# A two-layer encoder trunk on one core: the MLP's second product by seven block products instead of eight

## The chip, the core and the metric

The kernel runs on one NeuronCore of one Trainium2 chip. The metric is the time of one execution on the device in microseconds (us), the median of several runs. Engine names are those of the profile: PE is the matmul engine, PEld its weight loads, DVE the vector engine, ACT the scalar engine, POOL the general engine, SP the engine whose queue issues most transfers. Matmuls add up in eight banks of 128 x 512 floats, which the program names by the tiles `s` (two tiles of two banks), `pj` and `tp` (two banks each).

## What is computed

Two layers over 1024 tokens of width 1024, in 32-bit floats. Each layer has a mixer (layer 0: pooling and a gated recurrence; layer 1: chunked attention), a cross-attention into 256 memory tokens, and an MLP of width 4096, each between two RMSNorms. The change touches the MLP:

```python
def squared_relu_mlp(h, w1, w2):
    a = jax.nn.relu(h @ w1)
    return (a * a) @ w2
...
h = rmsnorm(x, g[4])
x = x + rmsnorm(squared_relu_mlp(h, w_ff1[l], w_ff2[l]), g[5])
```

Here h is 1024 x 1024, w1 is 1024 x 4096 and w2 is 4096 x 1024.

## The kernel before

**Products.** Operands go to PE in the type fp32r, and every operand is split into a high part (ACT casts it) and a low part (DVE subtracts the high part from the source), and one block product is three matmuls: high by high, high by low, low by high (`mm3`, L157; `split`, L170; `wsplit`, L120). All matmuls stand in the profile under L137. A tile of 128 x 1024 floats costs one cast and one subtraction.

**First product of the MLP** (`sevens`, L651). The 32 column tiles of w1 are taken in pairs n = 0 to 15. With the tokens in two halves and the inner dimension in two halves, a pair is a 2 x 2 by 2 x 2 block product. Pairs 1 to 15 are done by seven block products instead of eight (i = 0 to 6, in the order 0, 1, 3, 2, 5, 4, 6; Strassen's method in Winograd's form), each of 12 matmuls; pair 0 by eight (i = 7 to 14), while the sums of token blocks that the seven need are still being built. Those sums are made by `to_set` (L590) and `end_set` (L620) and lie in tiles `S` and, for one of them, in four tiles of the pool `a`. The list `seq` (L757 to L759) writes out the order by hand. `evac` (L738) is what empties the banks: ACT copies (L747), DVE adds (L754), and then relu and square either on ACT in two instructions (L749, L750) or on DVE in one (L755, for i = 1, 4 and 5). A finished pair is two tiles of 128 x 1024 in the pool `a`; ACT's queue writes them to device memory (`ffa`, L752).

**Second product** (L762 to L820). The 32 tiles f of the squared activation are read back in eleven blocks of 2, 3 (eight times), 2 and 4. For each f, `act` (L767) splits the activation tile into `ff` and `wsplit` splits the 128 rows of w2. For each of the eight row tiles tb, and each half n of the 1024 columns, the block's tiles are multiplied in one go, 3 matmuls per f. The result of a block goes by ACT copy (first block, L809) or DVE add (L811) into `y`, 8 tiles of 128 x 1024. In the last block, of four f, each row tile is finished at once: the sum of squares (L241), the gain (POOL, L242), the scale (POOL, L206 and L207), the residual (L244), the next norm (L213, L215) and, in layer 0, transposes for the next stage (L140). The last row tile of the program goes through `finish` (L249).

**What sets the order.** The kernel is written as a stream; a scheduler then orders each engine's instructions and gives out buffers from pools: `h8` (12 tiles of 8 KB per partition), `a` (15 tiles of 4 KB), `raw` (3), `w` (4) and `x` (5). A load waits in SP's queue until its buffer is free, and everything behind it waits too. `piece` (L143) fixes the order of PE's pieces.

## Time and profile before

| | |
|---|---|
| median of 3 runs | 2872.77 us (2872.22 to 2874.97) |
| the profiled execution | 2876.44 us, of which 2874.6 us are the span from the first to the last instruction |
| granted clock of PE, mean | 0.996 |
| PE busy, share of the span | 99% |
| first product of the MLP, layer 0 | from 688 us to 999.5 us |
| second product of the MLP, layer 0 | from 999.5 us to about 1352 us |
| second product of the MLP, layer 1 | from about 2517 us to 2865.2 us |

A group of instructions in the profile has the line, the engine, the operation, the tile written and the tiles read, the shapes and the count; then its busy time and the mean of one in ns; then the engine's idle time ahead of it and who ended it. A window lists the busy time of each engine in a stretch of the span, in brackets the number of instructions, then PE's granted clock, the share of the transfer engines' time and GB/s. Matmuls overlap, so the time of one is read from the distance between them.

### The profile page before, as it was taken

The numbers are of one execution on the slowest core, as the hardware profiler recorded it, in microseconds if no ns is written. First come the engines' busy times: TensorE is split into PE (matmuls) and PEld (weight loads), VectorE is DVE, ScalarE is ACT, GpSimd is POOL, SyncE is SP. The second block draws the span as 40 slices with busy tenths as digits, with TensorE's granted clock in tenths as the row PEclk, the third lists the DMA queues.
The fourth block names the chain that finished last, engine by engine and source line by source line (L and its number), as shares of the span: only waits on it lengthen the run. The fifth ranks groups of instructions, "written<-read, shape, count | busy, mean of one in ns | idle before, by whom it ended". The sixth has DMA issues, their size and how long they took to land.

```text
span 2874.6 us, 36400 instructions
## 1 busy us (share of the span) xinstructions
PE 2832.7 (99%) x13894; PEld 2375.2 (83%) x13894; DVE 1582.5 (55%) x2550; ACT 1131.8 (39%) x2174; POOL 620.3 (22%) x845
## 2 busy tenths in 40 slices
PE   9999999999999999999999999999999999999998
PEld 7888888888888888888888888878888888888887
DVE  4577733356755644555555556544255755645454
ACT  4344523443433421213555566633344433431111
POOL 2233413211000000005555555723211000000003
PEclk9999999999999999999999999999999999999999
DMA  7211632133333432332111111542033333442222
GB/s 194 60 33 35 190 133 88 44 114 114 121 114 118 164 122 88 101 108 92 54 38 38 39 47 44 155 141 96 30 118 115 127 110 104 151 155 88 88 88 88
DMA packets 173934, 283.68 MB, mean 99 GB/s; under 512 B 10416, under 2 KB 117552, under 8 KB 173760
## 3 DMA queue, kind: packets, MB, share of 16 engines
q1 hardware_dynamic: 162096, 243.35, 26.8%
q10 hardware_dynamic: 11664, 38.02, 3.5%
q8 instruction: 109, 1.79, 0.3%
q14 instruction: 65, 0.53, 0.1%
HBM read 214.74 MB, written 66.58 MB: 98 GB/s over the span
## 4 chain that ended last, share of the span: by engine, by line
PE 91%; DVE 3%; ACT 2%; POOL 2%; DMA 1%; issue 1%; SPq 0%; DVEq 0%; POOLq 0%; ACTq 0%
PE s L137 43%; PE pj L137 33%; PE tp L137 11%; PE tp L140 4%; DVE x L244 0%; POOL w L127 0%; DVE p L1180 0%; ACT a L125 0%; ACT zT L174 0%; DVE a L175 0%; ACT a L174 0%; POOL a L127 0%; POOL st L207 0%; POOL o L999 0%; DMA x<-in_w_o_att_dram 0%
## 5 line engine op out<-in xcount | busy, mean ns | idle before, releaser
L137 PE MATMUL pj<-hT,w 128*128 128x512 f32 x2640 | 656.0, 398 | 0.4 <-DVE hT L175 0.4
L137 PEld LDWEIGHTS pj<-hT,w 128*128 128x128 f32 x2640 | 481.6, 188 | 95.1 <-issue 1.9
L137 PE MATMUL s<-a,ff 128*128 128x512 f32 x2376 | 547.0, 389 | 0.4 <-ACT s L241 0.4
L137 PEld LDWEIGHTS s<-a,ff 128*128 128x128 f32 x2376 | 445.6, 188 | 93.8 <-ACT s L241 0.9
L137 PE MATMUL s<-S,w 128*128 128x512 f32 x1440 | 341.1, 389 | 0.0
L137 PEld LDWEIGHTS s<-S,w 128*128 128x128 f32 x1440 | 270.1, 188 | 56.3 <-ACT a L747 0.3
L137 PE MATMUL s<-a,zT 128*128 128x512 f32 x1280 | 308.9, 393 | 3.9 <-POOL a L127 3.3
L242 POOL TENSOR_TENSOR a<-y,x 128x1024 f32<-128x1024 f32 x15 | 41.8, 2786 | 1249.2 <-DVE y L811 1249.0
L137 PEld LDWEIGHTS s<-a,zT 128*128 128x128 f32 x1280 | 240.5, 189 | 56.3 <-POOL a L127 5.5
L811 DVE TENSOR_TENSOR y<-y,s 128x1024 f32<-128x1024 f32 x123 | 149.8, 1218 | 185.9 <-PE s L137 185.7
L127 POOL TENSOR_TENSOR w<-raw,w 128x1024 fp32r<-128x1024 f32 x75 | 185.7, 2477 | 240.9 <-ACT w L125 226.5
L770 ACT CAST ff<-x 128x1024 fp32r<-128x1024 f32 x52 | 53.0, 1051 | 322.8 <-PE s L137 321.1
L137 PE MATMUL pj<-a,ff 128*128 128x512 f32 x696 | 164.4, 389 | 0.0
L175 DVE TENSOR_TENSOR a<-tp,a 128x256 fp32r<-128x256 f32 (+2 forms) x272 | 113.5, 422 | 81.1 <-ACT a L174 77.0
L137 PEld LDWEIGHTS pj<-a,ff 128*128 128x128 f32 x696 | 130.7, 188 | 27.1
L125 ACT CAST w<-raw 128x1024 fp32r<-128x1024 f32 x92 | 96.6, 1050 | 130.4 <-PE pj L137 74.3
L137 PE MATMUL tp<-a,a 128*128 128x256 f32 (+1 forms) x1016 | 138.9, 279 | 5.9 <-DVE a L175 3.9
L137 PEld LDWEIGHTS tp<-a,a 128*128 128x128 f32 x1016 | 133.6, 191 | 13.0 <-DVE a L175 7.1
L1152 POOL TENSOR_SCALAR qd<-a 64x256 fp32r<-64x256 f32 x256 | 102.6, 401 | 149.3 <-PE s L137 134.7
L174 ACT CAST a<-tp 128x256 fp32r<-128x256 f32 (+2 forms) x272 | 99.5, 371 | 77.3 <-PE tp L140 47.7
L683 DVE TENSOR_TENSOR w<-a,w 128x512 fp32r<-128x512 f32 x124 | 85.6, 691 | 78.4 <-ACT w L682 78.2
L129 DVE TENSOR_TENSOR a<-raw,a 128x1024 fp32r<-128x1024 f32 x75 | 92.0, 1230 | 59.6 <-PE s L137 43.7
(227 smaller groups left out, 4094.7 us busy)
## 6 DMA issues: line engine op xcount, KB each, us to landing
raw<-in_w_ff_dram SPq DMA_DIRECT2D x96, 512.0 KB, 3.9
ffa<-a ACTq DMA_DIRECT2D x64, 512.0 KB, 2.8
x<-ffa SPq DMA_DIRECT2D x52, 512.0 KB, 5.1
xs<-x SPq DMA_DIRECT2D x40, 512.0 KB, 2.6
x<-xs SPq DMA_DIRECT2D x40, 512.0 KB, 3.4
raw<-in_w_mem_kv_dram SPq DMA_DIRECT2D x32, 512.0 KB, 4.1
x<-in_w_ff_dram SPq DMA_DIRECT2D x32, 512.0 KB, 3.8
raw<-in_w_qkv_dram SPq DMA_DIRECT2D x24, 512.0 KB, 4.0
```

Source lines behind the costliest of these rows:

```text
L125: nc.scalar.copy(h, raw)
L127: nc.gpsimd.tensor_tensor(l, raw, h, op=ALU.subtract)
L129: nc.vector.tensor_tensor(l, raw, h, op=ALU.subtract)
L137: self.lastpe = self.nc.tensor.matmul(*a, **k).ins
L140: self.lastpe = self.nc.tensor.transpose(out, in_, self.ident).ins
L174: nc.scalar.copy(hi, src)
L175: nc.vector.tensor_tensor(lo, src, hi, op=ALU.subtract)
L242: eng.tensor_tensor(yg, y, gpost, op=ALU.mult)
L683: nc.vector.tensor_tensor(w[:, 1], src, w[:, 0], op=ALU.subtract)
L770: nc.scalar.copy(t[:, 0], raw)
L811: nc.vector.tensor_tensor(yp, yp, pp, op=ALU.add)
L1152: nc.gpsimd.tensor_scalar(ts[-1][r * 64:r * 64 + 64, :], q[hd * 64:hd * 64 + 64, mp * 256:mp * 256 + 256], 1.0, 1.0, op0=ALU.mult, op1=ALU ...
```

## The change

**The second product** is done by seven block products for 28 of the 32 tiles f (14 pairs), and as before for the last four (`REST`). Tokens are halved (m), the 256 rows of w2 of a pair are halved, and the columns are halved. The new `seconds` runs 28 steps: four blocks of 2, 4, 4 and 4 pairs, and in each the seven products in the order 0, 2, 3, 1, 5, 4, 6. A step multiplies four row tiles j, one bank each, by one half of the columns, over all pairs of its block: 24 matmuls in the first block, 48 in the others. The stationary operand is a sum of activation blocks, the moving one a sum of blocks of w2.

**Sums.** Seven tiles `acc` of the pool `h8` hold the running sums from block to block. In each block products 0, 3 and 5 go on adding up in the same banks, and DVE adds those banks to the sums after each of the three (L809). For products 1, 2, 4 and 6, ACT copies the running sum into the banks before the step (L799) and out again after it (L812). In the first block ACT copies all seven out. In the last block DVE adds the sums up into the four quarters of the result, of which the last piece, with its four tiles f, reads a row tile where it read `y` before (L926).

**The activation sums** are made in the first product: at the end of each of the 14 pairs DVE does four more operations of 128 x 512 (L874), and four transfers instead of two write seven blocks of 128 x 512 instead of four (`ffd`, L871 to L877). Relu and square for i = 1 and 5 go from DVE to ACT (L860, L861). The list `seq` has `end_set` one product earlier, ahead of (0, 14).

**Operands of a step**: `load` (two steps ahead) reads one activation tile and, for four of the seven products, one w2 tile per two pairs; `split` (one step ahead) forms the difference of w2 blocks on DVE where there is one (L778) and splits both operands (L174, L175). The whole diff, less the part that removes the old loop and the argument `c` of `finish`:

```diff
+    BLOCKS = (0, 2), (2, 4), (6, 4), (10, 4)
+    REST = range(28, 32)
+    PLACE = 6, 0, 2, 3, 5, 4, 1
+    def seconds(self, W, ops_d, mid):
+        nc = self.nc
+        Wv = W.rearrange("(n q p) d -> p n q d", q=2, p=P)
+        steps = [(b, i) for b in range(len(self.BLOCKS)) for i in (0, 2, 3, 1, 5, 4, 6)]
+        raws, stage, tmp, ops, acc, banks = {}, {}, {}, {}, {}, {}
+        NEED = {0: (0, 0), 2: (0, 1), 3: (1, 1), 1: (1, 0)}
+        unit = (P, 2, 512)
+        def raw(tag, src):
+            if tag == "w":
+                t = self.wp.tile(list(unit), F32, tag="w", name=self.nm("w"))
+            else:
+                t = self.rawp.tile(list(unit), F32, tag="raw", name=self.nm("raw")) if tag == "raw" else self.act(tag, unit)
+            nc.sync.dma_start(t, src)
+            return t
+        def load(b, i):
+            n0, kb = self.BLOCKS[b]
+            if i in NEED:
+                q, m = NEED[i]
+                raws[b, q, m] = [raw(("x", "x", "w", "a")[2 * q + m], Wv[:, n0 + h:n0 + h + 2, q, m * 512:m * 512 + 512])
+                                 for h in range(0, kb, 2)]
+            stage[b, i] = [raw("raw", ops_d[(n0 + h) // 2][:, :, self.PLACE[i], :]) for h in range(0, kb, 2)]
+        def split(b, i):
+            kb = self.BLOCKS[b][1]
+            sh, sl = [self.h8([P, 4, 512], F32R, "sh") for _ in range(2)]
+            ops[b, i] = sh, sl, [], []
+            B = lambda q, m, h: raws[b, q, m][h]
+            for h in range(kb // 2):
+                if i == 2:
+                    tmp[b, h] = self.act("a", unit)
+                if i in (0, 1, 4):
+                    x = B(*{0: (0, 0), 1: (1, 0), 4: (1, 1)}[i], h)
+                else:
+                    x = self.act("a", unit) if i == 5 else tmp[b, h]
+                    y, z = {2: ((0, 1), (0, 0)), 3: ((1, 1), None), 5: ((1, 1), (0, 1)), 6: ((1, 0), None)}[i]
+                    nc.vector.tensor_tensor(x, B(*y, h), B(*z, h) if z else x, op=ALU.subtract)
+                for hi, lo, src in ((sh[:, 2 * h:2 * h + 2], sl[:, 2 * h:2 * h + 2], stage[b, i][h]),
+                                    (self.act("a", unit, F32R), self.act("a", unit, F32R), x)):
+                    self.split(hi, lo, src)
+                ops[b, i][2].append(hi)
+                ops[b, i][3].append(lo)
+        def run(k, b, i):
+            kb, last = self.BLOCKS[b][1], b == len(self.BLOCKS) - 1
+            chain = i in (0, 3, 5)
+            if i not in (3, 5):
+                two = [self.p2() for _ in range(2)] if k % 2 == 0 else [self.p1(p, t) for p, t in ((self.pj, "pj"), (self.tp, "tp")) * 2]
+                banks[k % 2] = two
+            w = 2 if k % 2 == 0 else 1
+            ps = [banks[k % 2][j // w][:, j % w * 512:j % w * 512 + 512] for j in range(4)]
+            wide = [t.rearrange("p (j d) -> p j d", j=w) for t in banks[k % 2]]
+            sums = lambda i: [acc[i][:, w * j:w * j + w, :] for j in range(4 // w)]
+            if b == 0:
+                acc[i] = self.h8([P, 4, 512], F32, "acc")
+            elif not chain:
+                for x, y in zip(wide, sums(i)):
+                    nc.scalar.copy(x, y)
+            sh, sl, th, tl = ops.pop((b, i))
+            first = i == 0 or (b == 0 and not chain)
+            for j in range(4):
+                sj = slice(j * P, j * P + P)
+                with self.piece():
+                    for n in range(kb):
+                        t = [x[n // 2][:, n % 2, :] for x in (th, tl)]
+                        for g, (v, m) in enumerate(((sh, t[0]), (sh, t[1]), (sl, t[0]))):
+                            self.mm(ps[j], v[:, n, sj], m, start=(first and n + g == 0), stop=(n == kb - 1 and g == 2), skip_group_check=not first)
+            add = lambda o, x, y: nc.vector.tensor_tensor(o, x, y, op=ALU.add)
+            for x, y in zip(wide, sums(i)):
+                if b == 0 or (not chain and not (last and i in (1, 4, 6))):
+                    nc.scalar.copy(y, x)
+                elif chain:
+                    add(y, y, x)
+            if last and i in (1, 4, 6):
+                for x, y, z in zip(wide, sums({1: 0, 4: 3, 6: 5}[i]), sums({1: 0, 4: 3, 6: 6}[i])):
+                    add(z, y, x)
+            if last and i in (3, 5):
+                for x, y, z in zip(sums(i), sums(2), sums({3: 3, 5: 2}[i])):
+                    add(z, x, y)
+        for k in range(2):
+            load(*steps[k])
+        split(*steps[0])
+        for k, (b, i) in enumerate(steps):
+            if k + 2 < len(steps):
+                load(*steps[k + 2])
+            if k + 1 < len(steps):
+                split(*steps[k + 1])
+            mid(len(steps) - k)
+            run(k, b, i)
+        return (acc[0], acc[3]), (acc[6], acc[2])
...
         W1, W2 = self.a["w_ff1"][l], self.a["w_ff2"][l]
-        act_d = [self.dp.tile([P, S], F32, name=f"ffa{l}_{f}") for f in range(32)]
+        act_d = {f: self.dp.tile([P, S], F32, name=f"ffa{l}_{f}") for f in self.REST}
+        ops_d = [self.dp.tile([P, 2, 7, 512], F32, name=f"ffd{l}_{m}") for m in range(self.REST[0] // 4)]
         o = {}
         def evac(n, i, ps):
@@ -748,74 +852,84 @@
             elif i in (6, 7, 9, 12, 14):
                 nc.scalar.activation(t, ps, AF.Relu)
                 nc.scalar.activation(t, t, AF.Square)
-                for c in range(2) if i in (6, 14) else ():
-                    nc.scalar.dma_start(act_d[2 * n + c], o.pop((n, c)).rearrange("p j t -> p (j t)"))
             else:
                 nc.vector.tensor_tensor(t, ps, t if i == 4 else o[n, 0][:, 1, :], op=ALU.add)
-                nc.vector.scalar_tensor_tensor(t, t, 0.0, t, op0=ALU.max, op1=ALU.mult)
+                if i == 4:
+                    nc.vector.scalar_tensor_tensor(t, t, 0.0, t, op0=ALU.max, op1=ALU.mult)
+                else:
+                    nc.scalar.activation(t, t, AF.Relu)
+                    nc.scalar.activation(t, t, AF.Square)
+            if i not in (6, 14):
+                return
+            o0, o1 = o.pop((n, 0)), o.pop((n, 1))
+            if 2 * n in self.REST:
+                for c, x in enumerate((o0, o1)):
+                    nc.scalar.dma_start(act_d[2 * n + c], x.rearrange("p j t -> p (j t)"))
+                return
+            d = ops_d[n // 2][:, n % 2]
+            s0, s1 = [self.act("a", (P, 2, 512)) for _ in range(2)]
+            nc.scalar.dma_start(d[:, 0:2], o1)
+            for x, y, z, op in ((s0[:, 0], o0[:, 1], o1[:, 1], ALU.add), (s1[:, 0], o0[:, 0], o0[:, 1], ALU.subtract),
+                                (s0[:, 1], s0[:, 0], o0[:, 0], ALU.subtract), (s1[:, 1], o1[:, 0], s0[:, 1], ALU.subtract)):
+                nc.vector.tensor_tensor(x, y, z, op=op)
+            nc.scalar.dma_start(d[:, 2:4], s0)
+            nc.scalar.dma_start(d[:, 4:6], s1)
+            nc.scalar.dma_start(d[:, 6], o0[:, 0])
         seq = [(0, 8), (0, 7), lambda: self.flush(len(self.pending) - 1), (0, 10), (0, 9), lambda: self.flush(), (1, 0), (1, 1)]
-        seq += [(2, 0), (2, 1)] + [(0, i) for i in range(11, 15)] + [lambda: self.end_set(A), (1, 2), (2, 2), (1, 3), (2, 3)]
+        seq += [(2, 0), (2, 1)] + [(0, i) for i in range(11, 13+1)] + [lambda: self.end_set(A)] + [(0, i) for i in range(13+1, 15)] + [(1, 2), (2, 2), (1, 3), (2, 3)]
         seq += [(1, 5), (2, 5), (1, 4), (1, 6), (2, 4), (2, 6)] + [(n, i) for n in range(3, 16) for i in (0, 1, 3, 2, 5, 4, 6)]
         self.sevens(W1, A, evac, seq)
...
+        fs = self.REST
+        def rest(f):
+            raw = self.wraw(act_d[f], (P, S), True)
+            if f == fs[-1]:
+                t = self.h8([P, 2, S], F32R, "ff")
+                a[f] = t[:, 0], t[:, 1]
+            else:
+                a[f] = [self.act("a", (P, S), F32R) for _ in range(2)]
+            self.split(*a[f], raw)
+            w2[f] = self.wsplit(W2[f * P:(f + 1) * P, :], (P, D), "w" if f == fs[1] else "a", "dve")
+        def mid(left):
+            for f in fs[:2] if left == 2 else fs[2:] if left == 1 else ():
+                rest(f)
+        C = self.seconds(W2, ops_d, mid)
...
+        for tb in range(NT):
+            if tb % 2 == 0:
+                y = self.h8([P, 2, D], F32, "y")
+            x = self.load_x(xsrc, tb)
+            tsl = slice(tb * P, tb * P + P)
+            fin = gpre is None and tb == NT - 1
+            ps = None if fin else self.p2()
+            ph = [ps[:, n * 512:n * 512 + 512] if ps is not None else self.p1(self.pj, "pj") for n in range(2)]
+            with self.piece():
+                for n in range(2):
+                    sl = slice(n * 512, n * 512 + 512)
+                    self.mm3(ph[n], [((a[f][0][:, tsl], a[f][1][:, tsl]), (w2[f][0][:, sl], w2[f][1][:, sl])) for f in fs])
+            yt = y[:, tb % 2, :]
+            c = [C[tb // 4][n][:, tb % 4, :] for n in range(2)]
+            if fin:
+                self.finish(ph, c, yt, x, tb, xdst, gpost)
+                break
+            for n in range(2):
+                nc.vector.tensor_tensor(yt[:, n * 512:n * 512 + 512], c[n], ph[n], op=ALU.add)
```

`order` of the built programs counts 10,654 matmuls of 512 columns before and 10,318 now; all other counts on PE are the same.

**Two places in the engines' order.** The first is DVE in layer 0, at the end of the operand sums of the first product. `L175` writing 128x2x128 is a split of the sum that product (1, 4) reads, `L634` and `L674` are sums, `L683` a split of w1, `w920` before and `w922` now that of (1, 4). Before:

```order
L634 TENSOR_TENSOR a913_5906<-a913_5906,S801_5156 128x512
L683 TENSOR_TENSOR w920_6009<-x865_5630,w920_6009 128x512
L175 TENSOR_TENSOR a910_5903<-a912_5905,a908_5901 128x2x128
L175 TENSOR_TENSOR a911_5904<-a912_5905,a909_5902 128x2x128
L674 TENSOR_TENSOR a929_6119<-raw880_5714 128x512
L683 TENSOR_TENSOR w922_6027<-a898_5840,w922_6027 128x512
L175 TENSOR_TENSOR a910_5903<-a913_5906,a908_5901 128x2x128
L175 TENSOR_TENSOR a911_5904<-a913_5906,a909_5902 128x2x128
L175 TENSOR_TENSOR a910_5903<-a913_5906,a908_5901 128x2x128
L175 TENSOR_TENSOR a911_5904<-a913_5906,a909_5902 128x2x128
L754 TENSOR_TENSOR a919_6007<-s2888_5758,a889_5771 128x512
```

The same place now, where `L874` are the new sums of pair 0 and `L856` is the add that was `L754`:

```order
L874 TENSOR_TENSOR a915_5935<-a874_5655 128x512
L634 TENSOR_TENSOR a912_5867<-a912_5867,S801_5156 128x512
L683 TENSOR_TENSOR w922_5998<-x865_5609,w922_5998 128x512
L175 TENSOR_TENSOR a909_5864<-a911_5866,a907_5862 128x2x128
L175 TENSOR_TENSOR a910_5865<-a911_5866,a908_5863 128x2x128
L683 TENSOR_TENSOR w924_6016<-a898_5821,w924_6016 128x512
L175 TENSOR_TENSOR a909_5864<-a912_5867,a907_5862 128x2x128
L874 TENSOR_TENSOR a914_5934<-a914_5934,a874_5655 128x512
L175 TENSOR_TENSOR a910_5865<-a912_5867,a908_5863 128x2x128
L856 TENSOR_TENSOR a921_5996<-s2888_5737,a889_5750 128x512
L175 TENSOR_TENSOR a909_5864<-a912_5867,a907_5862 128x2x128
L175 TENSOR_TENSOR a910_5865<-a912_5867,a908_5863 128x2x128
```

Three of the new sums (the first stands just above these rows) and one add now stand ahead of the last splits; two instructions of L755 and one of L674 that stood ahead are gone from there. Counted from the add that reads bank `pj` of product (1, 1) to the last of these splits there are 46 instructions of 128 x 512 and 8 small ones before, 47 and 8 now.

The second place is ACT in the middle of the second product of layer 0. Before, in the last blocks, it holds nothing but casts:

```order
L770 CAST ff1345_9577<-raw1344_9575 128x1024
L125 CAST a1347_9582<-raw1346_9580 128x1024
L770 CAST ff1350_9588<-raw1349_9586 128x1024
L125 CAST a1352_9593<-raw1351_9591 128x1024
L770 CAST ff1355_9599<-raw1354_9597 128x1024
L125 CAST a1357_9604<-raw1356_9602 128x1024
```

Now, in the third block: `sh` is the stationary operand of a step (`sh1323` that of product 1, which reads `w1307` and `w1308` too, `sh1331` that of product 5 after it), `acc1161` the sum of product 2, `acc1178` that of product 1, and the banks `pj1317`, `tp1318`, `pj1319`, `tp1320` of product 2 are the banks `pj1339` to `tp1342` of product 1:

```order
L174 CAST a1325_8974<-w1307_8884 128x1024
L174 CAST sh1323_8972<-raw1309_8888 128x1024
L174 CAST a1327_8980<-w1308_8886 128x1024
L812 COPY acc1161_8021<-pj1317_8908 128x512
L799 COPY pj1339_9058<-acc1178_8103 128x512
L174 CAST sh1323_8972<-raw1310_8890 128x1024
L812 COPY acc1161_8021<-tp1318_8909 128x512
L799 COPY tp1340_9059<-acc1178_8103 128x512
L812 COPY acc1161_8021<-pj1319_8910 128x512
L799 COPY pj1341_9060<-acc1178_8103 128x512
L812 COPY acc1161_8021<-tp1320_8911 128x512
L174 CAST sh1331_9040<-raw1321_8968 128x1024
```

Each bank's copy out and the copy of the next sum into it follow each other, bank by bank, and the casts for product 1 stand ahead of the last copies out of product 2, two steps before they are used.

68 lines of the change are left out of this document (13 added, 55 removed).

## Prediction

> **What bounds the kernel now.** First the page: the span, the busy times, and the shares of the chain that ended last.
>
> ```profile
> span 2874.6 us, 36400 instructions
> PE 2832.7 (99%) x13894; PEld 2375.2 (83%) x13894; DVE 1582.5 (55%) x2550; ACT 1131.8 (39%) x2174; POOL 620.3 (22%) x845
> GB/s 194 60 33 35 190 133 88 44 114 114 121 114 118 164 122 88 101 108 92 54 38 38 39 47 44 155 141 96 30 118 115 127 110 104 151 155 88 88 88 88
> PE 91%; DVE 3%; ACT 2%; POOL 2%; DMA 1%; issue 1%; SPq 0%; DVEq 0%; POOLq 0%; ACTq 0%
> ```
>
> PE is busy for 99% of the span and is 91% of the chain; no other engine is over 55%. But these are averages, so next the windows of the MLP: one pair of the first product, the second product up to its last block (layer 0), and the last block with what follows.
>
> ```profile
> core 0: us, PE busy (x) PEld busy (x) DVE busy (x) ACT busy (x) POOL busy (x), PEclk, DMA share, GB/s
> 768.04:787.08 19.04, 19.04 (x86) 15.77 (x85) 11.28 (x17) 6.82 (x12) 0.00 (x0) 1.00 0.34 111
> 996.79:1298.96 302.17, 302.17 (x1333) 250.00 (x1333) 155.74 (x149) 66.08 (x70) 0.00 (x0) 1.00 0.33 110
> 1298.96:1352.00 53.04, 52.65 (x248) 43.48 (x247) 28.47 (x28) 17.04 (x31) 31.58 (x28) 1.00 0.29 101
> ```
>
> In both products PE does not pause at all (302.17 of 302.17 us), its clock is granted in full (1.00), and DVE has 48% and ACT 78% of the second product free. So there a matmul that goes is worth its whole distance to the next, as long as the others keep up. That distance is read from the chain in order of time, where a stretch holds nothing but matmuls:
>
> ```profile
> 1007.67 5.44 PE s L137 x24
> 2816.20 43.53 PE s L137 x192
> ```
>
> 24 matmuls in 5.44 us and 192 in 43.53 us are 0.2267 us each (the 389 ns of a row is their length, overlap and all).
>
> **What PE saves.** Before: 8 row tiles by 2 halves by 32 f by 3 = 1536 matmuls per layer. Now: 14 pairs by 7 products by 4 row tiles by 3 = 1176, and 8 by 2 by 4 by 3 = 192 for the last four f: 1368. That is 168 less per layer, 336 in all, as in the built programs (10,654 less 10,318). 336 x 0.2267 = **76.2 us**. [...]
>
> **What the other engines get.** Durations, from the groups kept apart by shape:
>
> ```profile
> L811 DVE TENSOR_TENSOR y<-y,s 128x1024 f32<-128x1024 f32 x123 | 149.8, 1218 | 185.9 <-PE s L137 185.7
> L129 DVE TENSOR_TENSOR a<-raw,a 128x1024 fp32r<-128x1024 f32 x75 | 92.0, 1230 | 59.6 <-PE s L137 43.7 <-ACT a L125 15.8
> ...
> L771 DVE TENSOR_TENSOR ff<-x,ff 128x1024 fp32r<-128x1024 f32 x52 | 62.0, 1221 | 2.7 <-ACT ff L770 2.3
> L755 DVE SCALAR_TENSOR_TENSOR a<-a 128x512 f32<-128x512 f32 x90 | 61.6, 685 | 0.1
> ...
> L770 ACT CAST ff<-x 128x1024 fp32r<-128x1024 f32 x52 | 53.0, 1051 | 322.8 <-PE s L137 321.1 <-DMA x<-ffa 1.7
> ...
> L811 DVE TENSOR_TENSOR y<-y,pj 128x512 f32<-128x512 f32 x72 | 49.3, 687 | 64.8 <-PE pj L137 64.4
> ...
> L750 ACT ACTIVATE a<-a 128x512 f32<-128x512 f32 x38 | 24.1, 635 | 0.0
> ...
> L747 ACT COPY a<-tp 128x512 f32<-128x512 f32 x30 | 17.6, 588 | 45.5 <-issue 40.1 <-PE tp L137 5.4
> ...
> L241 ACT ACTIVATE s<-y 128x1024 f32<-128x1024 f32 x15 | 15.4, 1024 | 75.0 <-DVE y L811 75.0
> ```
>
> First product, per pair of 19.04 us: DVE gains four operations of 128 x 512 and gives up two of L755: 4 x 0.687 - 2 x 0.685 = +1.4, so 12.7 of 19.04 (67%). ACT takes over relu and square twice, 4 x 0.635 = +2.5, so 9.4 (49%). Both stay under PE, and what covers them is the slack of an engine that is 33% or more idle: they cost nothing. Two more writes per pair go through ACT's queue, where an issue takes:
>
> ```profile
> 747.00 0.33 ACTq L752 DMA_DIRECT2D ffa<-a  x1
> ```
>
> That is +0.7 us of ACT's time per pair (53% with it); behind them stand its casts of w1, made three products (8.2 us) ahead.
>
> The turn from pair 0 to the seven products is where DVE is tight, since the operand sums of `end_set` lie there. DVE and PE by time:
>
> ```profile
> 738.70 1.42 DVE L175 TENSOR_TENSOR a<-a,a 128x256 fp32r<-128x256 f32 x4
> 740.73 2.88 PE L137 MATMUL tp<-a,w 128*128 128x512 f32 x12
> ```
>
> The last four splits end at 740.12, and PE starts the product that reads them, (1, 4), at 740.73: 0.6 us to spare, and somewhat more, as its early matmuls read the first two. In the new order one more operation of 128 x 512 stands ahead of them (47 for 46, so +0.7 at most). I take 0.2 us per layer, between 0 and 0.7; not below 0, since PE does not wait there now.
>
> Second product, a block of four pairs: 7 x 48 matmuls, 76.2 us of PE. DVE: 28 low parts at 1.221, 8 differences at 1.230 and three adds of four banks at 2.44 (two of 1.218) to 2.75 (four of 0.687): 51.3 to 52.3 us, 67 to 69%. ACT: 28 casts at 1.051, four copies out and four in; a copy into banks has no row of its own, and L241 (`s<-y`, also from `y` into banks) with 1.024 per two banks and L747 with 0.588 per bank bound it: 2.05 to 2.35 per product, so 45.8 to 48.2 us, 60 to 63%. The block of two pairs: 38.1 us of PE; ACT has 14 casts and seven copies out, 29.1 to 31.2 us, **76 to 82%**, the fullest stretch of the change.
>
> Do the copies lie on PE's path? PE fills bank 0 in the first quarter of a step (2.72 of 10.88 us) and comes back to it two steps after the step's start: 19.0 us to carry out 1.2 us of copies; for the last bank it is the same. Where no copy in is made (first block), the four row tiles take 5.44 us a step, and a bank has 9.5 us. The order of ACT in the section on the change fits this: out and in follow bank by bank, the casts run ahead of them. I take 0, with the rivals below for the cover being gone.
>
> Transfers: a block of four pairs reads 14 activation and 8 w2 tiles of 512 KB, 11.5 MB in 76.2 us, 151 GB/s, for 110 in the window above and up to 194 in the page's slices. All are queued on SP in about the order of use, and steps are loaded two ahead (21.8 us); landings:
>
> ```profile
> raw<-in_w_ff_dram SPq DMA_DIRECT2D x96, 512.0 KB, 3.9
> ...
> x<-ffa SPq DMA_DIRECT2D x52, 512.0 KB, 5.1
> ```
>
> The pieces are 2 KB instead of 4, which no row prices; even at twice 5.1 us they land in time. I take 0.
>
> The end of each MLP: the last piece of four f is the same 192 matmuls, but its low half of the last w2 tile now stands on DVE between the last adds of sums, and a row tile takes two adds from `s` where one of 1218 did (2 x 0.687, +0.16 us). In layer 0 PE already waits there:
>
> ```profile
> 1340.00 5.76 PE L137 MATMUL s<-a,ff 128*128 128x512 f32 x24 [0.22 <-ACT s L241]
> 1346.80 5.74 PE L137 MATMUL s<-a,ff 128*128 128x512 f32 x24 [0.18 <-ACT s L241]
> ```
>
> so I add 0.16 for each of five row tiles, 0.8 us, in layer 0, and 0.3 us per layer for the turn into the last piece (0 to 1.2, one L129).
>
> **The sum.** -76.2 + 2 x 0.2 + 0.8 + 2 x 0.3 = -74.4 us. The profiled execution took 2876.44 us (span 2874.6 and 1.8 around it) and would take 2802.0. It is 3.7 us above the median of the runs, so the median goes from 2872.8 to **2798.4 us**. Its own bounds: 2794.5 (nothing lost, and a median 2 us lower in its spread, which is 2.8 us before) to 2804 (0.7 and 1.2 lost at the turns of both layers, the 0.8, and a median 2.8 us higher in its spread).
>
> **Rivals.**
>
> A, the gain is partly eaten in the block of two pairs. For: ACT at up to 82%, in order, with copies that wait for banks, so that casts behind a waiting copy come late. Against: 9.5 us per bank, and casts that run one or two steps ahead. Price: a copy of two banks ahead of a cast, 1.02 us exposed per step: 14.3 us over the 14 steps of the two small blocks, 28.7 us if as many later steps do the same. Less a gain of 74.4 us, the median is 2813 to 2827 us.
>
> B, slower: operands come too late in every step. `h8` has 12 tiles; seven hold sums, so 5 are left, two pairs and one tile. If the scheduler's order or a late landing makes the split of a step wait for the end of the step before, PE waits at each step for a cast, a low part and a bank's copy: 1.051 + 1.221 + 0.588 = 2.86 us, x 56 steps = 160 us, less 76.2: 2957 us. It decides from 76.2 / 56 = 1.36 us per step on. Against it: two full pairs are enough to prepare one while the other is read, and a step has 10.88 us for about 7 us of work on each engine.
>
> C, the first product slows down. The four sums stand on DVE between the adds that free PE's banks and the splits of w1. Price: one operation of 0.687 exposed in each of the 28 pairs, 19 us: 2818. Against: DVE is 33% idle there.
>
> That the change does not do what it says is closed: the matmuls are counted in the program.
>
> **How the numbers follow.** A measurement of this kernel can tell about 0.2% (5.7 us). Forecast as above (2794.5 to 2804): 0.77. A: 0.11. C: 0.06. B in full: 0.02, and 0.02 for enough of it to cancel the gain within 0.2%. A remainder of 0.02 is a gain beyond the count, to which no row points. The range runs from 2794 to 2818, which holds the forecast, the lower half of A and most of C, about 0.87: it ends where a loss of one operation per pair or a copy per small step would. Faster by over 0.2%: 0.96; within it 0.02; slower 0.02.
>
> **What would show it.** After: PE x13558 and about 2757 us busy; the stretch from the first product's end to the last piece about 267 us for 304.6 (1176 matmuls for 1344); in it PE without pauses, DVE 65 to 70% and ACT 60 to 65%; the first product's length unchanged. Wrong if waits of PE for L799, L174 or L175 sum to over 5 us per layer (A, B), if a pair of the first product takes more than 19.04 us (C), or if matmuls stand further apart than 0.2267 us.

## The result, and the profile after

The changed kernel takes 2802.61 us (median of 4 runs, 2801.2 to 2805.3), the kernel before on the same chip 2872.49 us (4 runs, 2870.98 to 2874.97). The ratio is 0.9757, 95% interval 0.974 to 0.9774: 69.9 us less, where 74.4 were forecast. The profiled execution of the changed kernel took 2805.3 us, that of before 2876.44: 71.1 us less.

The page after, with rows that answer to those of before:

```profile
span 2803.5 us, 36271 instructions
PE 2758.2 (98%) x13558; PEld 2314.7 (83%) x13558; DVE 1675.2 (60%) x2669; ACT 1393.7 (50%) x2518; POOL 617.9 (22%) x845
PE 89%; DVE 4%; ACT 2%; POOL 2%; DMA 1%; issue 1%; SPq 0%; DVEq 0%; POOLq 0%; ACTq 0%
```

PE lost 336 instructions and 74.5 us of busy time and is still the bound. DVE gained 92.7 us of work and ACT 261.9 us, neither of which lengthened the chain by its own length.

Next the windows of layer 0 in the changed kernel: the first product behind its turn (the passage from the eight products of pair 0 to the seven of the other pairs), the block of two pairs, the three blocks of four pairs, and all the steps of the second product together.

```profile
core 0: us, PE busy (x) PEld busy (x) DVE busy (x) ACT busy (x) POOL busy (x), PEclk, DMA share, GB/s
746.00:1001.00 255.00, 255.00 (x1126) 211.15 (x1126) 167.85 (x258) 128.83 (x216) 0.00 (x0) 1.00 0.47 165
1001.05:1039.00 37.95, 37.95 (x169) 31.43 (x168) 25.80 (x22) 30.24 (x39) 0.00 (x0) 1.00 0.68 228
1039.00:1267.60 228.60, 228.60 (x1010) 189.29 (x1009) 158.05 (x152) 128.79 (x146) 0.00 (x0) 1.00 0.45 147
1001.05:1267.62 266.57, 266.57 (x1178) 220.72 (x1177) 183.84 (x174) 159.03 (x184) 0.00 (x0) 1.00 0.48 159
```

and the same stretch of the second product before:

```profile
999.35:1303.99 304.64, 304.64 (x1344) 252.07 (x1343) 155.60 (x147) 66.08 (x70) 0.00 (x0) 1.00 0.32 106
```

PE is busy without a pause in every one of these rows. The second product shrank from 304.64 to 266.57 us, 38.07 per layer, which is 168 x 0.2266. So the gain is all there; what is missing lies outside. A ledger of the two profiled executions, from the starts of PE's groups in the timeline:

| stretch, us | before | after | difference |
|---|---|---|---|
| start to first product, layer 0 | 688.28 | 689.33 | +1.05 |
| first product, layer 0 | 311.07 | 311.72 | +0.65 |
| second product up to the last piece | 304.64 | 266.57 | -38.07 |
| last piece to the first product of layer 1 | 902.44 | 904.61 | +2.17 |
| first product, layer 1 | 310.16 | 311.72 | +1.56 |
| second product up to the last piece | 304.64 | 266.56 | -38.08 |
| last piece to the end | 53.37 | 52.99 | -0.38 |
| span | 2874.6 | 2803.5 | -71.1 |

The first row is code that the change does not touch; over the profiled executions of the changed kernel and its variants below it comes out between 685.99 and 689.33. The rest of the loss has two places. From the waits of PE after, in total, times and longest (the two larger ones above these rows, 4.6 and 3.8 us, were 5.8 and 3.9 before):

```profile
PE tp L140 <- DVE a L215: 3.5, 1, 3.5
PE s L137 <- ACT a L851: 2.5, 2, 1.2
...
PE s L137 <- ACT s L241: 2.0, 2, 1.0
```

The first of them is the start (1.4 before). The second is new, once per layer, at the turn. The third was 0.4 before and stands in the last piece of layer 0.

**The turn.** PE starts product (2, 5) 1.25 us late, and ACT shows why: the copy out of (2, 3), from whose bank that product goes on, is the last row here.

```profile
736.40 0.70 ACT L174 CAST a<-a 128x256 fp32r<-128x256 f32 x2
737.38 0.71 ACT L174 CAST a<-a 128x256 fp32r<-128x256 f32 x2 [0.27 <-DVE a L634]
738.64 0.62 ACT L682 CAST w<-x 128x512 fp32r<-128x512 f32 x1 [0.55 <-PE s L137]
739.17 0.58 ACT L851 COPY a<-s 128x512 f32<-128x512 f32 x1
```

```profile
739.80 3.02 PE L137 MATMUL s<-S,w 128*128 128x512 f32 x12 [1.25 <-ACT a L851]
```

Before, that copy ran ahead of the casts:

```profile
735.49 0.59 ACT L747 COPY a<-s 128x512 f32<-128x512 f32 x1 [1.00 <-PE s L137]
...
738.26 0.62 ACT L682 CAST w<-x 128x512 fp32r<-128x512 f32 x1 [0.44 <-PE s L137]
```

Now it stands behind casts of the operand sums, one of which waits 0.27 us for DVE, and directly behind that cast of w1 (L682). The cast waits until PE is done with the product before (2, 5), so PE then stands still for the cast and the copy: 0.53 us from the start of one to the start of the other, 0.58 us for the copy, and about 0.14 us between the engines. The wait for DVE is not the cause: in layer 1 no cast of an operand sum waits for DVE, and PE waits the same 1.25 us.

```profile
2221.54 0.62 ACT L682 CAST w<-x 128x512 fp32r<-128x512 f32 x1 [0.92 <-PE s L137]
...
2222.07 0.58 ACT L851 COPY a<-s 128x512 f32<-128x512 f32 x1
```

**The last piece of layer 0.** From its first matmul to the first matmul of the next projection (`pj<-hT,w`) it took 49.75 us before and takes 52.92 now. The timeline after, over a row tile and a half:

```profile
1292.01 0.68 DVE L926 TENSOR_TENSOR y<-acc,s 128x512 f32<-128x512 f32 x1
...
1292.60 0.68 DVE L175 TENSOR_TENSOR hT<-tp,hT 128x512 fp32r<-128x512 f32 x1
1292.77 2.40 POOL L242 TENSOR_TENSOR a<-y,x 128x1024 f32<-128x1024 f32 x1
...
1293.20 3.04 DVE L244 SCALAR_TENSOR_TENSOR x<-a,st,x 128x1024 f32<-128x1024 f32 x1
...
1296.16 0.68 DVE L175 TENSOR_TENSOR hT<-tp,hT 128x512 fp32r<-128x512 f32 x1
...
1296.77 1.27 DVE L926 TENSOR_TENSOR y<-acc,s 128x512 f32<-128x512 f32 x2
1296.90 0.66 PE L140 MATMUL tp<-ident,y 128*128 128x128 f32 x4 [0.59 <-DVE hT L175]
```

and the same place of a row tile before:

```profile
1328.43 1.21 DVE L811 TENSOR_TENSOR y<-y,s 128x1024 f32<-128x1024 f32 x1
...
1329.57 1.28 DVE L244 SCALAR_TENSOR_TENSOR x<-a,st,x 128x1024 f32<-128x1024 f32 x1
1329.73 3.38 POOL L242 TENSOR_TENSOR a<-y,x 128x1024 f32<-128x1024 f32 x1 [0.53 <-DVE y L811]
1330.76 1.28 DVE L175 TENSOR_TENSOR hT<-tp,hT 128x512 fp32r<-128x512 f32 x2
```

Before, DVE went from the add straight to the residual step L244, which was under way when POOL began its product with the gain, L242; POOL's product was the one that took longer, 3.38 us for 2.40. Now one L175 stands between the last add and L244. POOL begins first, and L244 takes 3.04 us instead of 1.28: it ends 1.07 us after POOL's end at 1295.17. What stands behind it on DVE (L175, the adds that free PE's banks) is late by as much, and PE waits. Over the eight row tiles of the last piece of layer 0 the traces show both orders. Now L244 begins while L242 runs in four of them; there it takes 2.83 to 3.40 us and ends 1.07 to 1.09 us after L242, and in the other four it takes 1.27 to 1.29. Before, L242 began 0.15 to 0.17 us after L244 in four of them and took 3.37 or 3.38 us, in the other four 2.38 to 2.41, and L244 took 1.27 to 1.29 in all eight. So of two that overlap, the one that started second took longer.

### The profile page after: what moved, and what is told of

Its sections match the earlier page's. It is cut to its first block, busy times and chain, and to the rows that moved or that the text cites. A ratio compares the mean times of both kernels' runs of the same rounds, so it can differ in the third digit from the quotient of the medians.

```text
span 2803.5 us, 36271 instructions
## 1 busy us (share of the span) xinstructions
PE 2758.2 (98%) x13558; PEld 2314.7 (83%) x13558; DVE 1675.2 (60%) x2669; ACT 1393.7 (50%) x2518; POOL 617.9 (22%) x845
## 2 busy tenths in 40 slices
DMA packets 207760, 327.73 MB, mean 117 GB/s; under 512 B 11984, under 2 KB 119120, under 8 KB 207584
## 4 chain that ended last, share of the span: by engine, by line
PE 89%; DVE 4%; ACT 2%; POOL 2%; DMA 1%; issue 1%; SPq 0%; DVEq 0%; POOLq 0%; ACTq 0%
PE s L137 37%; PE pj L137 33%; PE tp L137 16%; PE tp L140 4%; DVE x L244 1%; POOL w L127 1%; DVE p L1294 0%; DVE a L175 0%; ACT a L125 0%; ACT zT L174 0%; POOL a L242 0%; ACT a L174 0%; POOL st L207 0%; POOL a L127 0%; POOL o L1113 0%
## 5 line engine op out<-in xcount | busy, mean ns | idle before, releaser
L242 POOL TENSOR_TENSOR a<-y,x 128x1024 f32<-128x1024 f32 x15 | 39.8, 2652 | 1170.9 <-DVE y L926 1167.5
L137 PE MATMUL s<-a,sh 128*128 128x512 f32 x1152 | 265.7, 389 | 0.0
L137 PEld LDWEIGHTS s<-a,sh 128*128 128x128 f32 x1152 | 216.2, 188 | 44.9
L175 DVE TENSOR_TENSOR a<-tp,a 128x256 fp32r<-128x256 f32 (+2 forms) x272 | 113.3, 421 | 82.6 <-ACT a L174 78.8
L174 ACT CAST sh<-raw 128x1024 fp32r<-128x1024 f32 x98 | 102.5, 1052 | 90.4 <-DMA raw<-ffd 75.6
L137 PE MATMUL pj<-a,sh 128*128 128x512 f32 x600 | 145.1, 389 | 0.0
L137 PE MATMUL tp<-a,sh 128*128 128x512 f32 x600 | 145.1, 389 | 0.0
L175 DVE TENSOR_TENSOR a<-a,a 128x1024 fp32r<-128x1024 f32 (+1 forms) x86 | 91.8, 1071 | 79.1 <-ACT a L174 40.7
L174 ACT CAST a<-tp 128x256 fp32r<-128x256 f32 (+2 forms) x272 | 99.5, 371 | 77.8 <-PE tp L140 48.4
L137 PEld LDWEIGHTS pj<-a,sh 128*128 128x128 f32 x600 | 112.6, 188 | 23.4
L137 PEld LDWEIGHTS tp<-a,sh 128*128 128x128 f32 x600 | 112.6, 188 | 23.4
```

What stands on the lines that cost most here:

```text
L137: self.lastpe = self.nc.tensor.matmul(*a, **k).ins
L174: nc.scalar.copy(hi, src)
L175: nc.vector.tensor_tensor(lo, src, hi, op=ALU.subtract)
L242: eng.tensor_tensor(yg, y, gpost, op=ALU.mult)
```

## The experiments

Each was compared with the kernel before on its own chip. The changed kernel's ratio to it is 0.9757.

**One add per row tile.** The final sums get tiles that hold both halves of a row tile:

```
-            for n in range(2):
-                nc.vector.tensor_tensor(yt[:, n * 512:n * 512 + 512], c[n], ph[n], op=ALU.add)
+            r = lambda t: t.rearrange("p (n d) -> p n d", n=2)
+            nc.vector.tensor_tensor(r(yt), c, r(ps), op=ALU.add)
...
+                if i in (0, 2):
+                    t = [self.h8([P, 2, 2, 512], F32, "acc") for _ in range(2)]
+                    for n, z in enumerate({0: (0, 3), 2: (6, 2)}[i]):
+                        acc[z] = [x[:, n] for x in t]
```

> The four final sums are laid out so that both halves of a row tile lie in one tile, and the last piece takes one add of 128x1024 from PSUM per row tile instead of two of 128x512; the rest is as in the changed kernel. Theory (the two adds moved the hT low parts L175 ahead of the residual step L244 on DVE, so that L244 now starts after POOL's gain product L242 and is held until that ends): the DVE order is again add, L244, L175, L175, L215, every L244 of the last piece of layer 0 is 1.27 to 1.29 us (changed kernel: up to 3.4), the waits of PE for L241 and hT L175 there fall from 1.6 us at one place and 0.96 at another to under 0.5 in all, the granted clock does not dip to 0.5, and the way from the last piece of layer 0 to the next MLP is 901 to 902 us instead of 904.6: about 3 us faster than the changed kernel's 2802.6, 2799 to 2800. Rival (the last piece is late because sums of the second product and a w2 low part stand on DVE ahead of it, whatever the adds): nothing moves, 2802 to 2803.

Measured: 2797.54 us, ratio 0.9744 (0.9731 to 0.9758). The last piece takes 49.50 us, where the changed kernel and the seven runs below that keep both adds and the product on POOL take 52.50 to 52.92; DVE's order there is again add, L244, L175, L175, L215. The stretch to the next MLP, 902.17 us, decides nothing, since those same eight have it from 901.76 to 904.61. The total is 1.5 us below its range, and the start took 2.3 us less than in the changed kernel's profile. **The gain product on DVE** tests the same theory from the other side:

```
-            self.resid(yt, self.act("a"), yt, x, tb, xdst, gpost, gpre, ps, nc.gpsimd)
+            self.resid(yt, self.act("a"), yt, x, tb, xdst, gpost, gpre, ps, nc.vector)
```

> The product with the gain (L242) in the last piece of both MLPs goes from POOL to DVE; the two adds stay. Theory (DVE's L244 is held by POOL's L242): every L244 is 1.27 to 1.29 us although DVE has eight operations of 1.22 us more in layer 0; the stretch of DVE work grows by 9.8 us and loses about 9.6 us of holding, so DVE is as busy as before, 52 to 54 of 72 us; PE's waits for L241 and L175 fall by half at least; 2799.5 to 2802. Rival (DVE is simply late, because of the two adds and what stands ahead of them): with 9.8 us more on it, PE waits longer, 2805 to 2812.

Measured: 2794.3 us, ratio 0.9733 (0.9719 to 0.9746); the last piece takes 48.09 us. The interval of either run overlaps with that of the changed kernel, so what shows the gain is the last piece. The two operations in the last piece of layer 0 (busy, mean ns), first of the changed kernel, then with one add, then with the gain on DVE (here its first seven row tiles):

```profile
L242 POOL TENSOR_TENSOR a<-y,x 128x1024 f32<-128x1024 f32 x8 | 21.1, 2631 | 580.1 <-DVE y L926 579.4 <-issue 0.6
L244 DVE SCALAR_TENSOR_TENSOR x<-a,st,x 128x1024 f32<-128x1024 f32 x8 | 17.8, 2220 | 4.2 <-POOL st L207 4.0
```

```profile
L242 POOL TENSOR_TENSOR a<-y,x 128x1024 f32<-128x1024 f32 x8 | 23.1, 2888 | 583.7 <-DVE y L933 583.6
L244 DVE SCALAR_TENSOR_TENSOR x<-a,st,x 128x1024 f32<-128x1024 f32 x8 | 10.3, 1282 | 4.6 <-POOL st L207 4.6
```

```profile
L244 DVE SCALAR_TENSOR_TENSOR x<-a,st,x 128x1024 f32<-128x1024 f32 x7 | 9.0, 1285 | 2.5 <-POOL st L207 2.1
L242 DVE TENSOR_TENSOR a<-y,x 128x1024 f32<-128x1024 f32 x7 | 8.6, 1224 | 0.2
```

The mean of L244 goes from 2220 ns back to 1282, and with one add it is POOL that takes longer again (2888 for 2631). So the theory holds against "DVE is simply late": with 9.8 us more work on DVE the piece got faster, not slower. The size of the second run was underestimated. The gain product is itself a link of each row tile's chain, 1.22 us on DVE for 2.63 on POOL, and in layer 1, where no L175 competes, the end shrinks too, from 52.99 to 51.35 us. The two last pieces make up 6.5 of the 8.3 us by which this run lies below the changed kernel; the rest is in code that the edit does not touch.

**The operand sums (`end_set`) at their old place**, behind the whole of pair 0:

```
-[(0, i) for i in range(11, 13+1)] + [lambda: self.end_set(A)] + [(0, i) for i in range(13+1, 15)]
+[(0, i) for i in range(11, 15)] + [lambda: self.end_set(A)]
```

> The operand sums for the seven products (end_set) go back to their old place behind the whole of pair 0, everything else as in the changed kernel. Theory (the 1.25 us wait of PE at product (2,5) for ACT's copy out of (2,3) comes from the casts of the operand sums that now stand ahead of that copy): the wait for L851 goes at that place, and another of 0.4 to 3 us comes at product (1,4), since the last four splits of s4 follow later than in the changed kernel with four sums of pair 0 still ahead of them; between 2801 and 2807. Rival (the wait is due to the relu and square that ACT took over, not to the place of end_set): the wait of 1.25 for L851 stays, 2802 to 2803.

Measured: 2823.35 us, ratio 0.9834 (0.982 to 0.9847). The first product takes 323.17 us in layer 0 and 322.90 in layer 1, 11.4 and 11.2 more than in the changed kernel. PE, then DVE, then a window of that run at the turn:

```profile
733.71 0.79 PE L137 MATMUL s<-S,w 128*128 128x512 f32 x1 [6.19 <-ACT S L174]
738.46 12.97 PE L137 MATMUL s<-S,w 128*128 128x512 f32 x47 [3.95 <-DVE S L175]
```

```profile
723.26 0.69 DVE L683 TENSOR_TENSOR w<-a,w 128x512 fp32r<-128x512 f32 x1 [4.02 <-ACT w L682]
723.87 0.69 DVE L874 TENSOR_TENSOR a<-a,a 128x512 f32<-128x512 f32 x1
724.47 0.69 DVE L874 TENSOR_TENSOR a<-a 128x512 f32<-128x512 f32 x1
725.07 2.50 DVE L633 TENSOR_TENSOR a<-S,a 128x512 f32<-128x512 f32 x4
```

```profile
734.00:738.00 4.00, 0.51 (x1) 0.00 (x0) 4.00 (x8) 0.00 (x0) 0.00 (x0) 0.50 0.29 115
```

The wait for L851 is gone, as expected, but the expectation missed what took its place, and its size. The four new sums of pair 0 (L874) need its last activations, which come at 723.8; in DVE's order they stand ahead of `end_set`, so all of `end_set` (L633) begins only at 725.07, where it began at 713.11 in the changed kernel. PE stands for 10.1 us, and for part of the stretch behind it the granted clock is 0.50. **One product earlier**, between (0, 12) and (0, 13), was the attempt to mend the turn:

> The operand sums for the seven products stand one product of pair 0 earlier still, between (0, 12) and (0, 13); everything else as in the changed kernel. Theory (DVE runs in order: what of pair 0 stands ahead of the operand sums holds them up, by 10 us of PE in each layer at the old place, and by 1.25 us through ACT's copy out of (2, 3) at the place of the change): the wait for L851 falls from 1.25 us to 0 to 0.6 per layer, the first product takes 310.2 to 311.1 us per layer instead of 311.7; 2800 to 2803. Rival (the wait of 1.25 us is made by the casts of w1 and the copies of the seven products, which stay): 311.7 per layer stays, 2802 to 2804.

Measured: 2818.02 us, ratio 0.981 (0.9797 to 0.9824). The first product takes 319.65 and 318.55 us. PE at the turn of that run:

```profile
730.72 0.73 PE L137 MATMUL tp<-S,w 128*128 128x512 f32 x2 [3.54 <-ACT w L682]
735.02 4.35 PE L137 MATMUL tp<-S,w 128*128 128x512 f32 x10 [3.57 <-DVE w L683]
```

Now the operand sums are early and the weights are late: the differences and low parts of w1 (L680, L683) stand behind `end_set` on DVE. Neither forecast holds, though a cast of w1, which the rival names, is what the rows of the changed kernel show ahead of the copy; the place of the change is the only one of the three that leaves both in time, but for the 1.25 us.

**Relu and square of products 1 and 5 back on DVE:**

```
-                if i == 4:
-                    nc.vector.scalar_tensor_tensor(t, t, 0.0, t, op0=ALU.max, op1=ALU.mult)
-                else:
-                    nc.scalar.activation(t, t, AF.Relu)
-                    nc.scalar.activation(t, t, AF.Square)
+                nc.vector.scalar_tensor_tensor(t, t, 0.0, t, op0=ALU.max, op1=ALU.mult)
```

> Relu and square of products 1 and 5 go back from ACT to DVE (one operation of 0.685 us each for two of 0.635 on ACT), everything else as in the changed kernel. Theory (first product has room on both engines): the first product's stretch is unchanged within 0.5 us per layer away from the turn; DVE goes from 66 to about 73% and ACT from 50 to about 44% in it; the wait at the turn is 0 to 2.5 us. 2801 to 2805. Rival (the move was what kept DVE in time, the first product is tight): PE waits for L854-like adds or for the operands in many pairs, 0.2 us or more in each of 28, 2808 or more.

Measured: 2807.66 us, ratio 0.9774 (0.976 to 0.9787), a little above the theory's range. The first product takes 314.40 and 315.04 us, and behind the turn PE never waits. So the move to ACT is needed at the turn and shortly ahead of it. Ahead of it, in pair 0, PE waits 0.15 and 0.81 us for an add (L856). At the turn it waits 1.86 us, since there two casts of operand sums stand between the cast of w1 and the copy (0.61 us more), and then it runs at half its clock; in layer 1 of that run:

```profile
2223.65 4.61 PE L137 MATMUL s<-S,w 128*128 128x512 f32 x12 [1.86 <-ACT a L851]
```

```profile
2222.00:2224.00 2.00, 0.35 (x1) 0.30 (x2) 2.00 (x6) 1.60 (x4) 0.00 (x0) 0.99 0.47 129
2224.00:2226.00 2.00, 2.00 (x6) 1.63 (x5) 2.00 (x5) 0.00 (x0) 0.00 (x0) 0.50 0.83 313
2226.00:2228.00 2.00, 2.00 (x7) 1.55 (x7) 1.35 (x3) 0.00 (x0) 0.00 (x0) 0.66 0.87 232
```

**The matmuls given back**, with everything else of the change in place:

```
-                    for n in range(kb):
+                    for n in [*range(kb)] * (1 + (i == 6)):
```

> Product 6 of every block issues its matmuls twice, so that the second product has as many matmuls as before the change (1344 per layer and not 1176); the values of that product come out doubled. Everything else of the change stays. Theory (a matmul costs its distance of 0.2267 us and the rest of the change is hidden, but for about 4 us at the turns and in the last piece): 336 x 0.2267 = 76.2 us more than the changed kernel, 2878 to 2880, 5 to 8 us slower than the kernel before; the stretch of the steps is 304.7 us per layer. [...] Rival (part of the gain is eaten by the work on ACT and DVE in the steps): less than 76 us more, since the longer steps give that work its room back; 2872 or less.

Measured: 2877.47 us (10 runs), ratio 1.0018 (1.0009 to 1.0027), half a microsecond below the theory's range. The steps of layer 0:

```profile
998.35:1302.99 304.64, 304.64 (x1345) 252.25 (x1344) 183.41 (x174) 159.01 (x183) 0.00 (x0) 1.00 0.42 139
```

1344 matmuls in 304.64 us, as in the kernel before, though ACT has 2.4 times its work there and DVE 1.2 times. The whole program is 5.4 us above the kernel before: that is the price of all the rest of the change.

**Cover taken away.** Three runs load the engines that the prediction counted as covered.

```
-    BLOCKS = (0, 2), (2, 4), (6, 4), (10, 4)
+    BLOCKS = (0, 2), (2, 2), (4, 2), (6, 2), (8, 2), (10, 2), (12, 2)
```

> All blocks of the second product hold two pairs (seven blocks instead of four), so every step is 5.44 us of PE; ACT gets copies in and out per block: casts 14 x 1.05 and about 8 copies of two banks x 1.02 to 1.18 each way, 31 to 33 us of 38.1 (81 to 87%); DVE 14 low parts x 1.22, 4 differences x 1.23 and 3 x 2.44 to 2.75, 29 to 30 us (78%); loads the same. Theory (as long as no engine is full, the copies cost PE nothing; one bank has 9.5 us to be emptied and filled): the stretch is 266 to 272 us per layer, 2801 to 2814. Rival A of the prediction (a copy that waits for a bank stands ahead of a cast and is exposed, 1.02 us per step): in all 98 steps, 98 x 1.02 = 100 us, 2900.

```
-                    nc.scalar.copy(y, x)
+                    for _ in range(2):
+                        nc.scalar.copy(y, x)
```

> Every copy of a finished bank to its sum on ACT is made twice. ACT gets 1.01 us per two banks more: in the block of two pairs 7 steps x 2.03 = 14.2 us on 30.2 of 38.0, so 44.4 us, more than PE's 38.1; in a block of four pairs at most 4 x 2.03 = 8.1 us on about 43 of 76.2, so 67%. Theory (only the two-pair block becomes bound by ACT, its operands late by what is missing): PE waits 6 to 9 us per layer in that block and hardly beyond; 2815 to 2822. Rival (the order, not the load, decides; a copy exposed costs PE its length wherever it stands): 19 copies x 2.03 us x 2 layers = 77 us, 2880; or nothing at all, 2803, if ACT makes it up from the work done ahead.

```
-                nc.vector.tensor_tensor(x, y, z, op=op)
+                for _ in range(3):
+                    nc.vector.tensor_tensor(x, y, z, op=op)
```

> Each of the four operand sums per pair in the first product is computed three times: DVE gets 8 x 0.687 = 5.5 us more per pair of 19.04 us, from 66% to 95%. Theory (the sums lie under PE as long as DVE is not full, and the cover that they use is 6.3 us wide per pair): the first product grows by 0 to 0.3 us per pair, 0 to 8 us in 28 pairs, 2803 to 2811. Rival C of the prediction (a sum stands between the adds that free PE's banks and costs its length): 28 x 5.5 = 154 us if all of it shows, 2956; if one operation of 0.687 per repeated set shows, 38 us, 2841.

Measured, in this order: 2807.22 us, ratio 0.9771 (0.9757 to 0.9786); 2804.8 us (two executions near 2801 and two near 2808), 0.9767 (0.975 to 0.9783); 2806.02 us, 0.977 (0.9755 to 0.9784). A window of each at its fullest: two-pair blocks from the second on, the two-pair block with its copies out doubled, and the first product with the sums threefold.

```profile
1039.00:1230.00 191.00, 191.00 (x844) 158.22 (x843) 142.05 (x139) 151.13 (x189) 0.00 (x0) 1.00 0.45 141
```

```profile
998.54:1036.60 38.06, 37.55 (x166) 30.73 (x165) 25.82 (x22) 36.82 (x52) 0.00 (x0) 1.00 0.60 201
```

```profile
771.00:1001.00 230.00, 230.00 (x1016) 190.43 (x1015) 203.23 (x323) 116.20 (x196) 0.00 (x0) 1.00 0.47 167
```

ACT at 79% (151.13 of 191) through all blocks and DVE at 88% (203.23 of 230) cost PE nothing in these windows. The run with small blocks loses 2.8 us in layer 0 and 1.6 in layer 1, nearly all in the passage to the last piece, where PE waits 2.14 and 1.50 us for the last adds of sums. In the run with the sums threefold PE also waits once per layer behind the turn, at 764.93 in layer 0 and ahead of the window shown: 1.38 and 1.36 us for a low part of w1 (L683). Its first product is 2.1 us longer per layer. The doubled copies were misjudged: with 44 us of work for 38, ACT ran at 97% in the small block, and PE waited 0.51 us per layer, not 6 to 9; the steps are 0.88 us longer per layer. What ACT could not finish it carried into the next block, where it was busy for 28.86 of 38.40 us, against 21.12 in the changed kernel. The steps prepared ahead made up for it.

**The two remedies together, and two trials at the turn.** One add and the gain product on DVE:

> One add of 128x1024 per row tile and the gain product on DVE, both together, the rest as in the changed kernel. Theory (both remove the same holding of L244 by POOL; what the gain product on DVE brings beyond that is POOL's 2.4 us against DVE's 1.22 in the chain of every row tile): the last piece of layer 0 takes 47 to 48.1 us up to the next MLP-free projection (48.09 with the gain on DVE alone, 49.50 with one add alone, 52.92 in the changed kernel); 2792 to 2794.5. Rival (the two add up: 3.4 and 4.8): 44.7 us there, 2789 to 2791.

Measured: 2790.91 us (5 runs), ratio 0.9719 (0.9706 to 0.9732). The last piece takes 47.89 us (48.09 with the gain on DVE alone), so the two remove the same thing, as the theory said. The total came out below the theory's range and inside the rival's, but not by the rival's cause: the two last pieces give 6.7 us (5.0 and 1.7), and most of the rest lies behind the last piece of layer 0, in code that the edit does not touch. That code took 847.5 us up to the next MLP, and between 847.5 and 852.7 over all the profiled executions. This version is faster than both kernels: 11.7 us below the changed one, with intervals that do not touch. Its lead over the gain product on DVE alone lies inside the intervals. With the operand sums one product earlier as well:

> One add, the gain product on DVE, and the operand sums one product earlier. Theory: what the runs with the earlier operand sums and with the two others show, added up: 0 to 1.5 us per layer below one add with the gain on DVE; 2790 to 2794. Rival (the earlier place costs elsewhere, as the old place did): 2794 or more.

Measured: 2807.67 us, ratio 0.9775 (0.9761 to 0.9788). The first products are 7.7 and 6.8 us longer, so the rival holds. And with the one copy out of (2, 3) on DVE, in the version of the two remedies:

```
-            if i in (0, 2, 3):
+            if (n, i) == (2, 3):
+                nc.vector.tensor_copy(t, ps)
+            elif i in (0, 2, 3):
```

> One add, the gain product on DVE, and the one copy out of product (2, 3) on DVE instead of ACT (both take about 0.6 to 0.7 us). Theory (that copy waits on ACT behind casts of operand sums that wait for DVE): the wait of PE for L851 at product (2, 5) goes; but on DVE the copy stands behind the operand sums, so PE waits 0 to 2 us for it there; the first product takes 310.5 to 312.5 us per layer; 2791 to 2796. Rival (ACT's queue is the cause and nothing else): 310.5 per layer, 2790 to 2792.

Measured: 2800.34 us, ratio 0.9751 (0.9738 to 0.9764). PE waits 3.92 us for the copy in layer 0 and 2.82 in layer 1, where it waited 1.25 for ACT: the range for the wait (0 to 2 us) was too low, and ACT's queue is not the cause by itself. The first product took 315.97 and 314.88 us, above the range; in layer 0 the granted clock falls to 0.57 from 740 to 744 us, behind the wait, and twelve matmuls there take 4.43 us instead of 2.72. DVE is the tighter queue there: it is busy without a pause from 732 to 744 in the changed kernel. No run here removed the 1.25 us per layer without a longer wait in their place. What the rows point to, the copy ahead of that cast of w1 on ACT, was not tried.

## Why the prediction was right, and where its terms were off

The median of 2802.61 us is 4.2 us above the forecast of 2798.4 and within the bounds given with it.

**The saving** was right in count and price: 336 matmuls, 38.07 and 38.08 us per layer for 38.1 forecast, and PE x13558 with 2758.2 us for "about 2757". The run with the matmuls given back shows that nothing else in the change moves the second product.

**The other engines** came out as worked out. First product: DVE 66% (67 said) and ACT 51% (49 to 53). Second product: DVE 69% (67 to 69), ACT 60% over all steps (159.03 of 266.57; 60 to 63 said); in the two-pair block ACT 80% (76 to 82). The copies were priced at 0 and cost 0. That the cover was wide is now shown and not only argued: ACT can go to 97% in the small block, DVE to 88% in the first product, and the steps can be half as long, with 0.9 to 2.8 us per layer to pay.

**Transfers**: 147 GB/s in the four-pair blocks for 151 forecast, `raw<-ffd` lands in 4.8 us by the page after, and no wait of PE follows from them, though the program moves 327.73 MB instead of 283.68.

**The turn** was priced at 0.2 us per layer with bounds of 0 to 0.7. PE waits 1.25 us there in both layers, and the first products are 0.65 and 1.56 us longer. Layer 0 has the smaller figure in part because a wait of before is gone, 0.42 us at 718.83 for an add of pair 0 (L754), ahead of the place that the prediction followed. The place was right and the instruction wrong. DVE's last four splits were in time; ACT's copy out of (2, 3), queued behind a cast of w1 that waits for PE, was not. The prediction went through DVE's queue at this place and not through ACT's. Its own term was not put to the test: the splits end at 741.76, and the product that reads them starts at 742.66, but without the 1.25 us it would have started at 741.41. It also took the new place of `end_set` as a detail, while the runs at the other two places show that it decides over 11 us per layer on the one side and 7 to 8 on the other.

**The last piece** of layer 0 was priced at 0.8 us, by the longer adds, and cost 3.17 up to the next projection (2.17 up to the next MLP, as the code between took 1 us less in that execution). The longer adds were not it: with the gain on DVE, two adds per row tile and one differ by 0.2 us in the whole piece (48.09 against 47.89). Two adds instead of one changed the order on DVE, and the new order let POOL's product start ahead of L244, which then took up to 3.40 us instead of 1.28. With either remedy the mean of L244 in this piece is 1.28 again (1282 and 1285 ns). The passage into the last piece, priced at 0.3 us per layer, cost nothing: PE does not wait there.

**The rivals.** A (a copy exposed at every step of the small blocks), B (operands late at every step) and C (an operation exposed per pair) did not happen: PE does not wait at all in the steps, nor in the first product behind its turn. A needed far more than an ACT at 82%: at 97% it shows 0.51 us once per layer.

**The sum**: against 2802.0 for the profiled execution it came to 2805.3, 3.3 us more: +1.05 at the start, +1.8 in the two first products, +1.1 in the last piece and behind it in layer 0, -0.7 at the end of layer 1.

## What to carry to other kernels

Here PE was busy without pause in the second product while ACT was at 56 to 80% and DVE at 68 or 69%, and the count of the matmuls times their distance in the trace gave the saving: 38.1 us per layer said, 38.07 and 38.08 measured. Steps that are prepared one or two ahead absorbed even a stretch in which ACT had 44 us of work for 38, but for 0.51 us of waiting per layer. What the change lost, it lost at the turns between stages and in the last piece (1.25 us of waiting per layer at the turn, 3.17 us from the last piece of layer 0 to the next projection), so follow every engine's queue through each of them, in order, and not only the engine that looks tightest. When one operation becomes two of half the width, look at what will now stand between them and their successor, and which other engine then starts first.

## What the runs showed of the hardware beyond that

In some of these runs a short wait of PE was followed by a lower granted clock. In the changed kernel PE waited 0.59 and 1.02 us within 2.5 us in the last piece, and then its granted clock was halved for a while:

```profile
1296.00:1298.50 2.50, 0.97 (x7) 0.49 (x5) 2.10 (x5) 2.17 (x5) 0.74 (x2) 1.00 0.52 210
1298.50:1300.00 1.50, 1.42 (x5) 1.20 (x6) 1.50 (x2) 0.98 (x3) 1.31 (x2) 0.82 0.05 11
1300.00:1302.00 2.00, 2.00 (x6) 1.54 (x6) 1.88 (x2) 0.00 (x0) 2.00 (x2) 0.50 0.59 168
1302.00:1304.00 2.00, 2.00 (x9) 1.61 (x8) 2.00 (x2) 0.10 (x1) 0.73 (x1) 0.78 0.24 94
```

The shortfall from 1.00 adds up to 1.71 us (0.18 x 1.5 + 0.50 x 2 + 0.22 x 2), that is 3.42 us at half the clock; behind the wait of 1.86 us in the run with relu on DVE it is 3.40. The same two waits, at the same place, left the clock at 1.00 in six other runs (the operand sums at both other places, relu on DVE, two-pair blocks, copies out twice, sums threefold) and halved it again in the run with the matmuls given back. With the operand sums one product earlier, for one, the waits are 0.49 and 1.02 us, and the clock is 1.00 from 1304 to 1316 us. So waits of 1.61 us in all were followed by the halved clock in two runs, and one of 1.86 us in another, while waits of 1.25 us at the turn (changed kernel, 1.00 from 732 to 748 us) and of 1.38 us behind it (sums threefold) were not. What decides between the one and the other was not shown.

What the halved clock cost differed with what came next. In the last piece it was little: the two runs with the halved clock take 52.92 us for it, the six others 52.50 to 52.73, since these meet one more wait, of 0.95 to 0.98 us for L241 one row tile on, which the slower PE does not meet. In the first product nothing made up for it: with relu on DVE the two first products are 2.7 and 3.3 us longer than in the changed kernel, for waits that are 0.8 and 1.4 us longer.
